# The head of a two-layer backbone kernel: filler products, block copies on ScalarE, squares summed by TensorE

## Chip, cores, metric

The kernel runs on one core of a Trainium2 chip. The metric is the device time of one execution in microseconds, as a median over runs.

## What is computed

One inference step of a hybrid backbone: two layers, the same weights for 128 context tokens and 128 latent tokens. Each layer is a half-step SwiGLU network, three token-mixing branches, and another half-step SwiGLU network. What matters here is how the first of these begins:

```
mod = silu(cond) @ w_ada[l] + b_ada[l]          # shift, scale, gate: 9 x 1024 per group
h = rmsnorm(x, g[0]) * (1 + mod[1]) + mod[0]
x = x + 0.5 * mod[2] * swiglu(h, ffn_w_in[l, 0], ffn_w_out[l, 0])
```

Here cond is a vector of 1024 for each of the two groups, x is 256 x 1024, and ffn_w_in has 2 x 2816 columns.

## The kernel before, in words

Channels lie on partitions: x is eight channel tiles of 128 x 256 (256 tokens, two groups of 128). A weight tile is 128 output columns for all 1024 inputs, 128 x 1024 in f32, 512 KB. The products run in fp32r as three terms: a weight tile `raw` is split into a high part (`hi`, a cast on ScalarE, function emit_hi) and a low part (`lo`, a subtraction on VectorE, emit_lo), the activations too, and mm3 adds hi x hi, hi x lo and lo x hi. So one weight tile with eight channel tiles is 24 products of 128 x 258 (256 tokens and two columns that carry the shift). All weight tiles stream in one fixed sequence through four `raw` buffers; load_more issues them from SP's queue, and a load waits until the low part of the tile four places earlier is made. At most eight transfers are in flight, since each issue takes the semaphore of the eighth one before it.

The first SwiGLU network cannot start its products before the scale of a channel tile is known, which is a column of silu(cond) @ w_ada. That is the head (the code behind `load(cT, cT_d)`, from line 1686). The part of w_ada for scale and shift is cut into eight blocks of 1 MB (two buffers `big` from `wa`); block b holds scale and shift of channel tile b.

- All of x is loaded first, ScalarE squares it (xstat, tile `t1k`), VectorE adds the squares up in `sqa`, TensorE sums over partitions, VectorE, POOL and VectorE make the reciprocal root, and TensorE spreads it (norm_chain, rstd_diag, rstd_rows) into `rb`. `settle` puts this whole chain ahead of block 0 on TensorE's queue.
- block_mm(b): the block's products, silu(cond) as the stationary side, into the one accumulator `pa`; VectorE copies it to a `t1k` tile.
- block_feed(b): two selection products (`s<-cst,t1k`) turn the copied rows into columns; VectorE adds bias and one (`mods`), multiplies with the gain (`amod`) and writes the shift columns of the activations' high and low part; xfeed then makes the high part on ScalarE (`big<-x,amod`) and the low part on VectorE.
- Five weight tiles (T0) get an accumulator in the head already: three `pm` and two halves of `spare`. From step JOIN[t] on, tile t takes the products of those channel tiles whose feed is made (`done[t] <= step - 2`).

A step issues block_mm(step), then block_feed(step - 1), then the main products, up to channel tile step - 2, then the split of a further weight tile. Behind the ten steps, ffn_in goes on with the sixth weight tile. The list scheduler (class Pace) places side work there by modelled times; each engine runs its own instructions in the order in which they were issued.

Of the kernel before, what the change touches and what calls it, by code (L numbers as in the profile page):

```python
# [10 lines left out]
F32 = mybir.dt.float32  # L11
# [5 lines left out]
P = 128  # L17
D = 1024
# [22 lines left out]

ADA_DEPTH = 2
T0 = 5
JOIN = (0, 0, 3, 4, 5)
RAW_BUFS = 4
WH_BUFS = 5
WL_BUFS = 5
# [30 lines left out]
BR_LESS = (0, 0, 0, 0, 1, 1, 1, 1)  # L78
WO_LESS = (0, 0, 0, 0, 1, 1, 1, 1)
FO_LESS = (0, 0, 0, 0, 1, 1, 1)  # L80
LOADS = (2, 3, 4, 4)
PRE = 2
AHEAD = ("", "hl", "h", "lh", "")
T_SIDE = 3
T_SETUP = 6
YCUT = ((0, 2), (2, 2), (4, 2), (6, 2))
# [338 lines left out]
def backbone(ctx: ExitStack, tc: tile.TileContext, seq, wst, wada, wa0, wrow, xT_d, cT_d, cB_d, ck_d, cv_d, h0_d, prm_d, cst_d,  # L425
# [16 lines left out]
    def v3(t, a):  # L442
        return t.rearrange("p (a b) -> p a b", a=a)
# [14 lines left out]
    def tmp(tag, shape, dt=F32, bufs=None):  # L458
        return tp.tile(shape, dt, tag=tag, name=nm(tag), **({"bufs": bufs} if bufs else {}))
# [22 lines left out]
    def ps2():  # L482
        return grab("s2", pp.tile([P, 2, 512], F32, tag="s2", bufs=1, name=nm("s2")))
# [13 lines left out]
    def C(name):  # L497
        return cst[:, CST[name][0]:CST[name][1]]

    def R(l, name):  # L500
        return prm[l][:, PRM[name][0]:PRM[name][1]]
# [42 lines left out]
    def settle(cond):  # L544
        idle = 0
        while not cond():
            cand = [(s, lst) for lst, n in ((side["first"], 99), (side["gens"], CONC), (side["slow"], 99)) for s in lst[:n]]
            cand = [c for c in sorted(cand, key=lambda c: when(c[0]) - FIRST * (c[1] is side["first"])) if when(c[0]) < 1e8]
            idle = 0 if any(step_side(*c) for c in cand) else idle + 1
            assert idle < 3  # L550
# [7 lines left out]
    def misc(gen):  # L558
        add(gen, True)
# [5 lines left out]
    def load(out, src):  # L565
        nc.sync.dma_start(out=out, in_=src)
        pace.op("dma", out.free_size() * P * 4 / 360e3, [out], [])

    def load_more(limit):
        while st["load"] < min(limit, st["cap"]):  # L570
            i = st["load"]
            raws[i] = pace.slot("raw", RAW_BUFS, wp.tile([P, 1024], F32, tag="raw", bufs=RAW_BUFS, name=nm("raw")))
            load(raws[i], wst[i])
            st["load"] += 1
# [188 lines left out]
    def xstat(m):  # L763
        if m == 0:
            stat["acc"] = tmp("sqa", [P, NT], bufs=1)
            S.activation(out=stat["acc"], in_=x[:, 0], func=AF.Square)
            return lambda: None
        q = stat["sq"] = t1k()
        S.activation(out=q, in_=x[:, m], func=AF.Square)
        return lambda: V.tensor_tensor(out=stat["acc"], in0=stat["acc"], in1=q, op=ALU.add)  # L770

    def rstd_cols(ss, n, scale):
        v = tmp("rsv", [P, 8])
        V.tensor_scalar(out=v[:, :n], in0=ss, scalar1=scale, scalar2=EPS, op0=ALU.mult, op1=ALU.add)
        r = tmp("rsr", [P, 8])
        G.tensor_tensor(out=r[:, :n], in0=v[:, :n], in1=halfc[:, :n], op=ALU.pow)
        return r

    def rstd_diag(acc, scale, more=None):
        ps = ps1(2)  # L780
        for g in range(2):
            T_.matmul(ps[:, g:g + 1], lhsT=acc[:, g * P:(g + 1) * P], rhs=C("ones")[:, 0:1], start=True,
                      stop=more is None)
            if more is not None:
                T_.matmul(ps[:, g:g + 1], lhsT=more[:, g * P:(g + 1) * P], rhs=C("ones")[:, 0:1], start=False, stop=True)
        r = rstd_cols(ps, 2, scale)
        drop("s1", ps)
        dg = t1k()
        for g in range(2):
            V.tensor_scalar(out=dg[:, g * P:(g + 1) * P], in0=C("ident"), scalar1=r[:, g:g + 1], scalar2=None, op0=ALU.mult)  # L790
        return dg
# [10 lines left out]
    def norm_chain(box):  # L802
        yield "pe", stat["acc"], "s1"
        dg = rstd_diag(stat["acc"], 1.0 / D)
        yield "pe", dg, "s1"
        box["rb"] = rstd_rows(dg)
# [19 lines left out]
    def xfeed(m):  # L826
        l, n = feed["ln"]
        hi, lo = feed["hs"][m]
        if FEED_ACT and m < FEED_ACT:
            f = t1k()  # L830
            for g in range(2):
                sl = slice(g * P, (g + 1) * P)
                S.activation(out=f[:, sl], in_=x[:, m, sl], func=AF.Copy, scale=Amod[l][:, n, m, g:g + 1])
            S.copy(hi[:, :NT], f)
            return lambda: V.tensor_tensor(out=lo[:, :NT], in0=f, in1=hi[:, :NT], op=ALU.subtract)
        for g in range(2):
            sl = slice(g * P, (g + 1) * P)
            S.activation(out=hi[:, sl], in_=x[:, m, sl], func=AF.Copy, scale=Amod[l][:, n, m, g:g + 1])

        def finish():  # L840
            for g in range(2):
                sl = slice(g * P, (g + 1) * P)
                V.scalar_tensor_tensor(out=lo[:, sl], in0=x[:, m, sl], scalar=Amod[l][:, n, m, g:g + 1], in1=hi[:, sl],
                                       op0=ALU.mult, op1=ALU.subtract)
        return finish
# [811 lines left out]
    def ssd_norm(l, yv, yh, yl, box):  # L1657
# [25 lines left out]
            V.scalar_tensor_tensor(out=box["ts"][m], in0=box["ts"][m], scalar=1.0, in1=rb[:, :NT], op0=ALU.add, op1=ALU.mult)  # L1683
        box["done"] = True

    load(cT, cT_d)
    load(x, xT_d)
    load(cst[:, 0:CST_E], cst_d[:, 0:CST_E])
    load(prm[0], prm_d[0, :, 0:PRM_R])
    V.memset(silc, 0.0)  # L1690
    V.memset(halfc, -0.5)
    S.activation(out=silc[:, :, 0:2], in_=cT, func=AF.Silu)
    blocks = []

    def block_load():
        blocks.append([big(), big()])
        for h in range(2):
            load(blocks[-1][h], wa0[len(blocks) - 1, h])

    def split():  # L1700
        emit_hi()
        emit_lo()

    for n in LOADS[:-1]:
        load_more(n)
        block_load()
    load_more(LOADS[-1])
    feed_open(0, 0)
    for m in range(KD):
        xstat(m)()  # L1710
    box = {"rb": None}
    misc(norm_chain(box))
    split()
    split()
    settle(lambda: box["rb"] is not None)
    evs = {}

    def block_mm(b):
        ps = pada()
        for k in range(KD):  # L1720
            j = k % 4
            T_.matmul(ps[32 * j:32 * j + 32, :], lhsT=silc[:, k, :], rhs=blocks[b][k // 4][:, j * NT:(j + 1) * NT],
                      start=(k < 4), stop=(k >= 4))
        evs[b] = t1k()
        V.tensor_copy(evs[b], ps)
        blocks[b] = None

    def block_feed(b):
        ev = evs.pop(b)
        pt = ps1(4)  # L1730
        for h in range(2):
            T_.matmul(pt[:, 2 * h:2 * h + 2], lhsT=ev[:, h * P:(h + 1) * P], rhs=C("sel"), start=True, stop=True)
        sc = mods[0][:, 1, b, :]
        V.tensor_scalar(out=sc, in0=pt[:, 0:2], scalar1=R(0, "bada")[:, KD + b:KD + b + 1], scalar2=1.0, op0=ALU.add,
                        op1=ALU.add)
        sh = mods[0][:, 0, b, :]
        V.tensor_scalar(out=sh, in0=pt[:, 2:4], scalar1=R(0, "bada")[:, b:b + 1], scalar2=None, op0=ALU.add)
        drop("s1", pt)
        V.tensor_scalar(out=Amod[0][:, 0, b, :], in0=sc, scalar1=R(0, "gain")[:, b:b + 1], scalar2=None, op0=ALU.mult)
        hi, lo = feed["hs"][b]  # L1740
        V.tensor_copy(hi[:, NT:], sh)
        V.tensor_tensor(out=lo[:, NT:], in0=sh, in1=hi[:, NT:], op=ALU.subtract)
        xfeed(b)()

    spare = ps2()
    pre, ws = [], []
    done = {}
    for step in range(KD + 2):
        if step < KD:
            block_mm(step)  # L1750
            if len(blocks) < KD:
                block_load()
                if len(blocks) == KD:
                    st["cap"] = len(seq)
                    load_more(st["lo"] + RAW_BUFS)
        if 1 <= step <= KD:
            block_feed(step - 1)
        for t in range(T0):
            if step < max(2, JOIN[t]):
                continue  # L1760
            if t == len(pre):
                ws.append(tiles8(use(("fin", 0, 0, (t % 2) * KF + t // 2))))
                pre.append(pmain(NT + 2) if t < 3 else spare[:, t - 3, 0:NT + 2])
                done[t] = 0
            while done[t] <= step - 2:
                k = done[t]
                mm3(pre[t], ws[t][k:k + 1], feed["hs"][k:k + 1], k == 0, k == KD - 1)
                done[t] += 1
        if st["lo"] < T0 and step + 2 >= JOIN[st["lo"]]:
            split()  # L1770
        if step >= KD - 3:
            for what in AHEAD[step - KD + 3]:
                what = emit_hi() if what == "h" else emit_lo()
    while st["lo"] < T0 + PRE:
        if st["hi"] == st["lo"]:
            emit_hi()
# [54 lines left out]
```

## Time and profile before

| | |
|---|---|
| runs | 1559.09 us median of 3 (1557.94 to 1559.66) |
| the profiled execution's own time | 1558.1 us |
| its span | 1556.3 us |
| TensorE busy | 1524.8 us, 98% |
| VectorE busy | 1303.8 us, 84% |
| ScalarE busy | 863.2 us, 55% |
| bytes moved | 348.26 MB, 224 GB/s over the span |

PE is TensorE's products and PEld its weight loads, DVE is VectorE, ACT is ScalarE, SP is the queue that issues the transfers. Names such as `pm<-big,wh` read output<-inputs by the program's tiles, buffer numbers left out; all compute instructions have line 394, since a helper there records them. An f32 product (not fp32r) appears as several records, so a block's eight products are 16 records, two selection products four. The time of a busy TensorE is modelled at its ends, so from start to start is a safer measure than a duration.

### The profile page before, as it was taken

Reading aid. Unit: us, or ns where it says so; the run is one execution under the profiler, and the core shown is the slowest. Engines: PE = TensorE matmul, PEld = TensorE weight load, DVE = VectorE, ACT = ScalarE, POOL = GpSimd, SP = SyncE. Lnnn points to the kernel's source line nnn. Section 1 sums busy time; section 2 is a strip of 40 time slices with the busy share of each in tenths; the row PEclk is TensorE's granted clock in tenths of the full one; section 3 lists DMA queues with packets and bytes.
Section 4 is the critical chain, followed back from the end, with each engine's and each line's share of the span. In section 5 each row is a group of like instructions: output and inputs, shape, how many; then the busy total and the mean of one; then the engine's idle time right before and its main releaser. Section 6 shows DMA issues by size and latency. Waiting matters only on the chain.

```text
span 1556.3 us, 30558 instructions
## 1 busy us (share of the span) xinstructions
PE 1524.8 (98%) x11950; PEld 1429.2 (92%) x11950; DVE 1303.8 (84%) x2404; ACT 863.2 (55%) x1560; POOL 60.7 (4%) x65
## 2 busy tenths in 40 slices
PE   5999999999999999999999999999999999999997
PEld 4988889989989999899899998998898999999986
DVE  5777698986888988888989899898779899888754
ACT  3564447665577446644447544577556754565442
POOL 0000002000001000000001000110000010010000
PEclk9999999999999999999999999999999999999998
DMA  9688774554755666688765877555466567568652
GB/s 372 219 328 298 262 268 163 189 188 129 247 207 182 216 231 231 214 281 297 258 217 197 292 276 269 192 177 182 151 218 212 177 206 264 171 202 284 222 180 81
DMA packets 98736, 348.26 MB, mean 224 GB/s; under 512 B 10912, under 2 KB 14624, under 8 KB 98464
## 3 DMA queue, kind: packets, MB, share of 16 engines
q1 hardware_dynamic: 98592, 346.31, 65.2%
q8 instruction: 94, 1.54, 0.4%
q14 instruction: 50, 0.41, 0.1%
HBM read 342.07 MB, written 4.19 MB: 222 GB/s over the span
## 4 chain that ended last, share of the span: by engine, by line
PE 80%; issue 11%; DVE 5%; DMA 2%; ACT 1%; POOL 0%; DVEq 0%; POOLq 0%; SPq 0%
PE pm L394 72%; PE s L394 6%; DMA big<-wada 2%; PE pa L394 2%; DVE big L394 1%; DVE t1k L394 1%; DVE wl L394 1%; ACT big L394 1%; DVE wide L394 0%; DMA x<-xT 0%; ACT wh L394 0%; DVE sqa L394 0%; ACT L394 0%; POOL osr L394 0%; ACT rb L394 0%
## 5 line engine op out<-in xcount | busy, mean ns | idle before, releaser
L394 PE MATMUL pm<-big,wh 128*128 128x256 f32 (+2 forms) x6568 | 1294.1, 294 | 3.6 <-DVE big L394 2.1
L394 PEld LDWEIGHTS pm<-big,wh 128*128 128x128 f32 x6568 | 1029.8, 189 | 52.8 <-issue 20.2
L394 PE MATMUL pm<-big,wl 128*128 128x256 f32 (+1 forms) x3592 | 1004.9, 281 | 0.0
L394 PEld LDWEIGHTS pm<-big,wl 128*128 128x128 f32 x3592 | 676.6, 188 | 2.4
L394 DVE TENSOR_TENSOR wl<-raw,wh 128x1024 fp32r<-128x1024 f32 x481 | 586.2, 1223 | 9.4 <-ACT wh L394 8.9
L394 ACT CAST wh<-raw 128x1024 fp32r<-128x1024 f32 x481 | 501.5, 1047 | 136.9 <-PE pm L394 97.8
L394 DVE SCALAR_TENSOR_TENSOR big<-big,big 128x1024 f32<-128x1024 f32 x198 | 241.2, 1218 | 13.4 <-DMA big<-wrow 11.7
L394 ACT CAST big<-t1k 128x256 fp32r<-128x256 f32 x88 | 35.8, 407 | 155.8 <-DVE t1k L394 155.8
L394 PE MATMUL pm<-wh,big 128*128 128x512 f32 x256 | 89.0, 410 | 0.0
L394 ACT ACTIVATE big<-x,amod 128x128 fp32r<-128x128 f32 x96 | 33.4, 395 | 96.2 <-DVE x L394 77.8
L394 DVE TENSOR_TENSOR wide<-pm,rb 128x258 f32<-128x258 f32 (+1 forms) x108 | 45.1, 421 | 38.8 <-PE pm L394 32.9
L394 DVE SCALAR_TENSOR_TENSOR x<-pm,mods,x 128x128 f32<-128x128 f32 x152 | 43.5, 343 | 35.7 <-PE pm L394 35.7
L394 ACT COPY big<-pm 128x256 f32<-128x256 f32 (+2 forms) x88 | 31.0, 373 | 56.6 <-PE pm L394 55.9
L394 PEld LDWEIGHTS pm<-wh,big 128*128 128x128 f32 x256 | 48.1, 188 | 13.2 <-issue 2.3
L394 DVE TENSOR_TENSOR big<-t1k,big 128x256 fp32r<-128x256 f32 x128 | 55.5, 437 | 1.6 <-ACT big L394 0.9
L394 ACT ACTIVATE t1k<-wide 128x128 f32<-128x128 f32 (+1 forms) x96 | 33.4, 395 | 37.7 <-DVE wide L394 37.7
L394 PE MATMUL pm<-wl,big 128*128 128x512 f32 x128 | 50.6, 395 | 0.0
L394 ACT ACTIVATE t1k<-pm 128x256 f32<-128x256 f32 x58 | 22.3, 385 | 47.3 <-PE pm L394 47.2
L394 PE MATMUL s<-big,big 128*64 128x128 f32 (+5 forms) x416 | 46.4, 312 | 0.0
L394 POOL TENSOR_TENSOR rsr<-rsv,halfc 128x2 f32<-128x2 f32 x9 | 6.3, 698 | 917.5 <-DVE rsv L394 917.5
L394 DVE SCALAR_TENSOR_TENSOR big<-big,cw,big 128x252 f32<-128x252 f32 (+1 forms) x96 | 39.3, 472 | 2.6 <-ACT big L394 2.5
L394 PEld LDWEIGHTS s<-big,big 128*128 128x128 f32 (+2 forms) x416 | 35.3, 172 | 5.5 <-issue 3.3
(150 smaller groups left out, 970.4 us busy)
## 6 DMA issues: line engine op xcount, KB each, us to landing
raw<-wst SPq DMA_DIRECT2D x486, 512.0 KB, 4.3
big<-wrow SPq DMA_DIRECT2D x96, 512.0 KB, 5.7
big<-wada SPq DMA_DIRECT2D x32, 512.0 KB, 5.8
big<-wa SPq DMA_DIRECT2D x16, 512.0 KB, 10.1
big<-cB SPq DMA_DIRECT2D x12, 512.0 KB, 7.3
x<-xT SPq DMA_DIRECT2D x1, 1024.0 KB, 5.1
big<-h SPq DMA_DIRECT2D x2, 512.0 KB, 5.1
ns<-t SPq DMA_DIRECT2D x8, 128.0 KB, 3.7
```

The lines of the kernel that those rows point to most:

```text
L394: r = fn(*a, **k)
```

## The change

It rewrites the head. The norm's chain is no longer ahead of block 0. Instead the squares of x are made one or two at a time behind the blocks' feeds (table XSTAT), and TensorE sums each over partitions with a ones column into one accumulator `pq`; the root and its spreading come at steps 7 and 8. A step now issues block_mm(b), main products up to channel tile b - 1, the selection and feed of the same block b, then squares and their ones products, then products of a zero tile into an accumulator that is not read (table WARM: 13 ahead of block 0, then 9, 6 and 2). The copy of the accumulator moves from VectorE to ScalarE. Shift and scale get their bias in one VectorE operation, and one plus scale is taken inside the product with the gain. x is loaded in four pieces between the blocks (ORDER), the parameters ahead of them. Weight tiles join at steps 1, 2, 3, 7 and 8.

```diff
-JOIN = (0, 0, 3, 4, 5)
-LOADS = (2, 3, 4, 4)
-AHEAD = ("", "hl", "h", "lh", "")
+JOIN = (1, 2, 3, 7, 8)
+ORDER = "wxrwxrwxrwx wr wr w w".split()
+WARM = (13, 9, 6, 2)
+XSTAT = {1: (0,), 2: (1, 2), 3: (3, 4), 4: (5,), 5: (6,), 6: (7,)}
+AHEAD = {6: "h", 7: "l", 8: "hl"}
...
+    zero = tmp("t512", [P, 512], F32R)
+    V.memset(zero.bitcast(F32), 0.0)
     load(cT, cT_d)
-    load(x, xT_d)
+    load(prm[0], prm_d[0, :, 0:PRM_R])
     load(cst[:, 0:CST_E], cst_d[:, 0:CST_E])
-    load(prm[0], prm_d[0, :, 0:PRM_R])
...
+    spare = ps2()
+
+    def warm(n):
+        for _ in range(n):
+            T_.matmul(spare[:, 1, :], lhsT=zero[:, 0:P], rhs=zero, start=True, stop=True)
...
-    for m in range(KD):
-        xstat(m)()
     box = {"rb": None}
-    misc(norm_chain(box))
-    split()
-    split()
-    settle(lambda: box["rb"] is not None)
...
         evs[b] = t1k()
-        V.tensor_copy(evs[b], ps)
+        S.copy(evs[b], ps)
...
-    def block_feed(b):
+    def block_feed(b, lo_too):
...
-        sc = mods[0][:, 1, b, :]
-        V.tensor_scalar(out=sc, in0=pt[:, 0:2], scalar1=R(0, "bada")[:, KD + b:KD + b + 1], scalar2=1.0, op0=ALU.add,
-                        op1=ALU.add)
-        sh = mods[0][:, 0, b, :]
-        V.tensor_scalar(out=sh, in0=pt[:, 2:4], scalar1=R(0, "bada")[:, b:b + 1], scalar2=None, op0=ALU.add)
+            T_.matmul(pt[:, 2 - 2 * h:4 - 2 * h], lhsT=ev[:, h * P:(h + 1) * P], rhs=C("sel"), start=True, stop=True)
+        sh, sc = mods[0][:, 0, b, :], mods[0][:, 1, b, :]
+        V.tensor_tensor(out=mods[0][:, 0:2, b, :], in0=v3(pt, 2),
+                        in1=R(0, "bada").rearrange("p (i k) -> p i k", k=KD)[:, 0:2, b:b + 1].to_broadcast([P, 2, 2]), op=ALU.add)
         drop("s1", pt)
-        V.tensor_scalar(out=Amod[0][:, 0, b, :], in0=sc, scalar1=R(0, "gain")[:, b:b + 1], scalar2=None, op0=ALU.mult)
+        V.scalar_tensor_tensor(out=Amod[0][:, 0, b, :], in0=sc, scalar=1.0, in1=R(0, "gain")[:, b:b + 1].to_broadcast([P, 2]),
+                               op0=ALU.add, op1=ALU.mult)
...
-        xfeed(b)()
+        later = xfeed(b)
+        if lo_too:
+            emit_lo()
+        later()
...
+    pq = ps1(2)
+    warm(WARM[0])
+    for step in range(KD + 1):
+        if step < KD:
+            block_mm(step)
+            if step + 1 < len(ORDER):
+                head_load(ORDER[step + 1])
...
+        joined(step)
+        if step == KD:
+            box["rb"] = rstd_rows(dg)
+            for t in range(len(pre)):
+                mains(t, KD - 1)
+        for t in range(len(pre)):
+            mains(t, step)
+        if step == KD - 1:
+            dg = diag(pq, 1.0 / D)
+        if step < KD:
+            if step < T0:
+                emit_hi()
+            block_feed(step, step < T0)
+            for m in XSTAT.get(step, ()):
+                q = t1k()
+                S.activation(out=q, in_=x[:, m], func=AF.Square)
+                for g in range(2):
+                    T_.matmul(pq[:, g:g + 1], lhsT=q[:, g * P:(g + 1) * P], rhs=C("ones")[:, 0:1], start=(m == 0 and g == 0),
+                              stop=(m == KD - 1), skip_group_check=True)
+        if step + 1 < len(WARM):
+            warm(WARM[step + 1])
```

The function mains(t, n) issues mm3 for weight tile t up to channel tile n - 1; joined(step) gives tile t its accumulator once step has reached JOIN[t]; diag is the second half of rstd_diag.

How the order on an engine moves is read at two places. First TensorE, in the middle of the head. Before, from the products of block 5 (`pa`, eight products in two rows) on: `s_359` is the selection of block 4, and the `pm` rows are main products of weight tiles 0, 1 and 2 with channel tile 3.

```order
L394 MATMUL pa_348<-big_223,silc 32x256 x4
L394 MATMUL pa_348<-big_224,silc 32x256 x4
L394 MATMUL s_359<-cst,t1k_304 128x2 x2
L394 MATMUL pm_239<-big_113,big_140 128x258
L394 MATMUL pm_239<-big_115,big_140 128x258
L394 MATMUL pm_239<-big_113,big_142 128x258
L394 MATMUL pm_243<-big_113,big_146 128x258
L394 MATMUL pm_243<-big_115,big_146 128x258
L394 MATMUL pm_243<-big_113,big_148 128x258
```

The same engine in the change: the second row of block 5's products, the nine main products of channel tile 4, block 5's own selection (`128x2`) and the ones products of a square (`128x1`).

```order
L396 MATMUL pa_377<-big_192,silc 32x256 x4
L396 MATMUL pm_197<-big_122,big_156 128x258
L396 MATMUL pm_197<-big_124,big_156 128x258
L396 MATMUL pm_197<-big_122,big_167 128x258
L396 MATMUL pm_241<-big_122,big_201 128x258
L396 MATMUL pm_241<-big_124,big_201 128x258
L396 MATMUL pm_241<-big_122,big_212 128x258
L396 MATMUL pm_295<-big_122,big_251 128x258
L396 MATMUL pm_295<-big_124,big_251 128x258
L396 MATMUL pm_295<-big_122,big_262 128x258
L396 MATMUL s_397<-cst,t1k_386 128x2 x2
L396 MATMUL s_125<-cst,t1k_408 128x1 x2
```

The selection has moved from ahead of the main products to behind them and belongs to the same block as the products above; the ones products are new, and the next block's products follow them.

Second ScalarE, in the middle of the head. Before, between the spreading of the norm and block 4's feed (`big<-x,amod` is a feed, `big<-raw` a weight tile's high part):

```order
L394 COPY rb_162<-s_160 128x256
L394 ACTIVATE big_113<-x,amod_84 128x128 x2
L394 CAST big_208<-raw_101 128x1024
L394 ACTIVATE big_113<-x,amod_84 128x128 x2
L394 CAST big_247<-raw_107 128x1024
L394 ACTIVATE big_113<-x,amod_84 128x128 x2
L394 CAST big_291<-raw_144 128x1024
L394 ACTIVATE big_113<-x,amod_84 128x128 x2
L394 ACTIVATE big_114<-x,amod_84 128x128 x4
```

In the change, from block 4's copy to block 6's square (`t1k<-pa` is a copy of the accumulator, `t1k<-x` a square):

```order
L396 COPY t1k_345<-pa_336 128x256
L396 CAST big_356<-raw_195 128x1024
L396 ACTIVATE big_122<-x,amod_84 128x128 x2
L396 ACTIVATE t1k_373<-x 128x256
L396 COPY t1k_386<-pa_377 128x256
L396 ACTIVATE big_122<-x,amod_84 128x128 x2
L396 ACTIVATE t1k_408<-x 128x256
L396 COPY t1k_421<-pa_412 128x256
L396 ACTIVATE big_122<-x,amod_84 128x128 x2
L396 ACTIVATE t1k_443<-x 128x256
```

The copies are new on this engine, and each square stands behind the feed of its block and ahead of the next block's copy.

## Rows read from the trace of the kernel before

**Rows 1.** The page: busy time, share of the span and instructions of each engine.

```profile
PE 1524.8 (98%) x11950; PEld 1429.2 (92%) x11950; DVE 1303.8 (84%) x2404; ACT 863.2 (55%) x1560; POOL 60.7 (4%) x65
```

**Rows 2.** The chain of waits in order of time, 0 to 110 us: start, us, what.

```profile
1.18 5.14 DMA x<-xT
...
10.62 1.22 DVE big L394 x2
...
15.62 1.91 PE pa L394 x16
...
26.11 1.23 DVE big L394
27.34 0.35 DVE t1k L394
...
47.03 20.33 PE pm L394 x168
```

**Rows 3.** The timeline of TensorE, 10 to 47 us: start, us, engine, line, operation.

```profile
10.76 1.01 PE L394 MATMUL s<-cst,sqa 128*128 128x1 f32 x4 [10.76 <-DVE sqa L394]
14.39 1.22 PE L394 MATMUL s<-t1k,cst 128*128 128x256 f32 x2 [2.63 <-DVE rb L394]
15.55 1.94 PE L394 MATMUL pa<-big,silc 128*32 128x256 f32 x16
18.03 1.68 PE L394 MATMUL pa<-big,silc 128*32 128x256 f32 x16 [0.55 <-DVE t1k L394]
...
24.08 1.07 PE L394 MATMUL pa<-big,silc 128*32 128x256 f32 x16 [1.27 <-DVE t1k L394]
...
39.49 1.07 PE L394 MATMUL pa<-big,silc 128*32 128x256 f32 x16
40.49 0.61 PE L394 MATMUL s<-cst,t1k 128*128 128x2 f32 x4
40.96 1.33 PE L394 MATMUL pm<-big,big 128*128 128x258 f32 x9
42.12 0.88 PE L394 MATMUL s<-big,big 128*128 128x258 f32 x6
42.84 0.50 PE L394 MATMUL s<-cst,t1k 128*128 128x2 f32 x4
...
46.87 0.41 PE L394 MATMUL pm<-big,wh 128*128 128x258 f32 x2
```

**Rows 4.** The timeline of VectorE, one block's feed.

```profile
43.38 0.34 DVE L394 TENSOR_SCALAR mods<-s,prm 128x2 f32<-128x2 f32 x2 [0.44 <-PE s L394]
43.64 0.22 DVE L394 TENSOR_SCALAR amod<-mods,prm 128x2 f32<-128x2 f32 x1
...
44.33 0.64 DVE L394 SCALAR_TENSOR_TENSOR big<-x,amod,big 128x128 fp32r<-128x128 f32 x2 [0.21 <-ACT big L394]
44.89 1.22 DVE L394 TENSOR_TENSOR wl<-raw,wh 128x1024 fp32r<-128x1024 f32 x1
46.02 0.42 DVE L394 TENSOR_TENSOR wide<-pm,rb 128x258 f32<-128x258 f32 x1
```

**Rows 5.** The timeline of ScalarE: squares, a copy from the accumulator, a feed, a cast.

```profile
6.66 2.37 ACT L394 ACTIVATE t1k<-x 128x256 f32<-128x256 f32 x7
...
15.65 0.37 ACT L394 COPY rb<-s 128x256 f32<-128x256 f32 x1 [4.74 <-PE s L394]
...
43.89 0.69 ACT L394 ACTIVATE big<-x,amod 128x128 fp32r<-128x128 f32 x2 [0.41 <-DVE amod L394]
44.49 1.03 ACT L394 CAST wh<-raw 128x1024 fp32r<-128x1024 f32 x1
```

**Rows 6.** Three windows: us, busy time of each engine, granted clock, DMA share, GB/s.

```profile
0.00:10.00 10.00, 0.00 (x0) 0.00 (x0) 2.67 (x8) 5.13 (x12) 0.20 (x4) 1.00 0.79 283
10.00:20.00 10.00, 6.07 (x42) 2.98 (x42) 4.06 (x10) 1.29 (x2) 0.70 (x1) 1.00 1.03 415
20.00:30.00 10.00, 8.21 (x88) 5.92 (x87) 7.46 (x27) 4.89 (x9) 0.00 (x0) 1.00 1.02 413
```

**Rows 7.** The timeline of SP's queue: the first issue behind eight transfers that waits for the fifth.

```profile
8.50 1.60 SPq L566 DMA_DIRECT2D big<-wa  x2
```

More of the change, by code (lines that the diff above doesn't have):

```diff
@@ L785, in rstd_diag, with diag @@
                 T_.matmul(ps[:, g:g + 1], lhsT=more[:, g * P:(g + 1) * P], rhs=C("ones")[:, 0:1], start=False, stop=True)
+        return diag(ps, scale)
+    def diag(ps, scale):
         r = rstd_cols(ps, 2, scale)
@@ L1692, in backbone @@
     S.activation(out=silc[:, :, 0:2], in_=cT, func=AF.Silu)
+    spare = ps2()
+    def warm(n):
+        for _ in range(n):
+            T_.matmul(spare[:, 1, :], lhsT=zero[:, 0:P], rhs=zero, start=True, stop=True)
     blocks = []
+    xs_in = [0]
     def block_load():
@@ L1702, in split, with head_load @@
         emit_lo()
[L1704 to L1707, printed above, removed]
+    def head_load(items):
+        for c in items:
+            if c == "w":
+                block_load()
+            elif c == "x":
+                i = xs_in[0]
+                load(x[:, i:i + 2], xT_d[:, i:i + 2])
+                xs_in[0] = i + 2
+            else:
+                st["cap"] += 1
+                load_more(st["cap"])
+    st["cap"] = 0
+    head_load(ORDER[0])
     feed_open(0, 0)
-    for m in range(KD):
-        xstat(m)()
     box = {"rb": None}
-    misc(norm_chain(box))
-    split()
-    split()
-    settle(lambda: box["rb"] is not None)
     evs = {}
@@ L1731, in block_feed @@
         for h in range(2):
-            T_.matmul(pt[:, 2 * h:2 * h + 2], lhsT=ev[:, h * P:(h + 1) * P], rhs=C("sel"), start=True, stop=True)
-        sc = mods[0][:, 1, b, :]
-        V.tensor_scalar(out=sc, in0=pt[:, 0:2], scalar1=R(0, "bada")[:, KD + b:KD + b + 1], scalar2=1.0, op0=ALU.add,
-                        op1=ALU.add)
-        sh = mods[0][:, 0, b, :]
-        V.tensor_scalar(out=sh, in0=pt[:, 2:4], scalar1=R(0, "bada")[:, b:b + 1], scalar2=None, op0=ALU.add)
+            T_.matmul(pt[:, 2 - 2 * h:4 - 2 * h], lhsT=ev[:, h * P:(h + 1) * P], rhs=C("sel"), start=True, stop=True)
+        sh, sc = mods[0][:, 0, b, :], mods[0][:, 1, b, :]
+        V.tensor_tensor(out=mods[0][:, 0:2, b, :], in0=v3(pt, 2),
+                        in1=R(0, "bada").rearrange("p (i k) -> p i k", k=KD)[:, 0:2, b:b + 1].to_broadcast([P, 2, 2]), op=ALU.add)
         drop("s1", pt)
-        V.tensor_scalar(out=Amod[0][:, 0, b, :], in0=sc, scalar1=R(0, "gain")[:, b:b + 1], scalar2=None, op0=ALU.mult)
+        V.scalar_tensor_tensor(out=Amod[0][:, 0, b, :], in0=sc, scalar=1.0, in1=R(0, "gain")[:, b:b + 1].to_broadcast([P, 2]),
+                               op0=ALU.add, op1=ALU.mult)
         hi, lo = feed["hs"][b]
@@ L1742, in block_feed, with joined @@
         V.tensor_tensor(out=lo[:, NT:], in0=sh, in1=hi[:, NT:], op=ALU.subtract)
-        xfeed(b)()
-    spare = ps2()
+        later = xfeed(b)
+        if lo_too:
+            emit_lo()
+        later()
     pre, ws = [], []
     done = {}
[L1748 to L1757, printed above, removed]
+    def joined(step):
         for t in range(T0):
-            if step < max(2, JOIN[t]):
+            if step < JOIN[t]:
                 continue
@@ L1764, in backbone, with mains @@
                 done[t] = 0
[L1765 to L1773, printed above, removed]
+    def mains(t, upto):
+        while done[t] < upto:
+            k = done[t]
+            mm3(pre[t], ws[t][k:k + 1], feed["hs"][k:k + 1], k == 0, k == KD - 1)
+            done[t] += 1
+    pq = ps1(2)
[5 more added lines that the diff above has]
+                head_load(ORDER[step + 1])
+                if len(blocks) == KD:
+                    st["cap"] = len(seq)
+                    load_more(st["lo"] + RAW_BUFS)
+        joined(step)
[19 more added lines that the diff above has]
+            warm(WARM[step + 1])
+        for what in AHEAD.get(step, ""):
+            what = emit_hi() if what == "h" else emit_lo()
     while st["lo"] < T0 + PRE:
```

## The prediction

> **What bounds the kernel now.** I read the page first: TensorE is busy 98% of the span [rows 1]. Then the chain of waits in order of time, to see where the other 2% lie [rows 2]: up to 47 us it changes engine all the time (input transfer, VectorE, TensorE), and from 47.03 on it is TensorE without a break, 168 products of a weight tile in 20.33 us. So the kernel is a head of 47 us and a body that TensorE alone sets. The order of the instructions on all engines is the same in both kernels behind the head (TensorE's sixth weight tile is the first common piece). So I compare one mark: the start of the sixth tile, 46.87 us [rows 3]. What the mark gains or loses, the kernel gains or loses.
>
> The head is eight blocks, and how often a block comes round is read from TensorE's timeline [rows 3]: block 0 at 15.55, block 7 at 39.49, that is 3.42 us each. A block's evacuation, its selection products and its feed overlap the next block there: the selection of block b-1 stands behind the products of block b, and TensorE runs on without waiting for the feed it has just set off.
>
> **The change, part by part.** The blocks' order on TensorE becomes: products of block b, main products of channel tile b-1, selection of block b, ones products of the squares, products of block b+1. The ones products wait for a square that ScalarE makes *behind* block b's feed, and the feed waits for VectorE's scale, which waits for the selection. Nothing is pipelined any more, and one round is the sum of its parts:
> - products of a block to the next instruction: 1.00 (39.49 to 40.49 [rows 3]);
> - nine main products: 40.96 to 42.12, 1.16 [rows 3];
> - selection to VectorE's first operation: 42.84 to 43.38, 0.54 [rows 3, 4];
> - VectorE's scale and shift: 43.38 to ScalarE's start at 43.89 is 0.51 with three operations [rows 4, 5]; the change has two, about 0.13 less with a wider first one, so I take 0.42;
> - ScalarE's feed until the next instruction starts: 43.89 to 44.49, 0.60; a square, 0.40 (seven in 2.37 are 0.33 from start to start, and the last one's end) [rows 5];
> - hand-over to TensorE 0.06 (the gaps between a product's end and its reader are of this size), and the ones products, the same form as the selection but for one column, 0.60 until the next block.
>
> Sum: 1.00 + 1.16 + 0.54 + 0.42 + 0.60 + 0.40 + 0.06 + 0.60 = **4.78 us** a round, against 3.42 before. It counts for blocks 2 to 7 (rounds 1 to 6 have squares).
>
> *Start.* The norm of all of x leaves the front, where it held block 0 until 15.55. Now block 0 waits for its own load: 1.33 MB lie ahead of its end, with 0.28 MB of it small inputs. By 10 us 283 GB/s have brought 2.83 MB, then it is 415 GB/s [rows 6]. Block 1 ends at 3.16 MB: 10.8 us. The queue's issue at 8.50 waited for the fifth transfer (1.85 MB, due at some 7.6 by these rates) [rows 7], so landings come 0.8 us behind the byte count: 11.6. Whether block 0's products run cold (1.94) or warm (1.00) [rows 3] changes nothing, since they begin near 7 and block 1 is not there before 11.6. So the 13 filler products at the start, and the nine after block 0, I cost at nothing: the load of block 1 hides them.
>
> *Block 2.* The first square stands behind feed 1, which stands behind the cast of the second raw tile: 3.95 MB, 12.7 + 0.8 = 13.5; cast 1.03, feed 0.60, square 0.40, hand-over and ones 0.66 give 16.2; six fillers of 512 columns at 1.16 / 9 x 512 / 258 = 0.26 give 17.7. *Block 3:* 4.78 + a second square and pair of ones (0.33 + 0.14) + two fillers 0.5 = 5.75: 23.5. *Block 4:* 15 main products for nine (+0.77), two squares (+0.47): 6.0: 29.5. *Blocks 5 to 7:* 3 x 4.78: **43.8** for block 7, against 39.49. Its load is not what it waits for: 12.34 MB ahead of its end, 2.83 + 4.15 by 20 us, the other 5.36 at 413 GB/s: 33.0, with 0.8 added 33.8.
>
> *End.* Behind block 7: its products 1.00, main products of the three joined tiles (9), of tile 3 (21), selection 0.5, the product that spreads the norm 0.6 (1.22 for it before, cold [rows 3]), tile 4 (21), the last channel of all five (15). 66 x 20.33 / 168 = 8.0, in all 10.1 us. The mark falls at **53.9**, where the old tail took 46.87 - 39.49 = 7.4: tiles 3 and 4 joined at steps 4 and 5 and now join at 7 and 8. Hidden in it: feed 7 (0.42 + 0.69 + 0.64 [rows 4, 5]) behind tile 4's 2.5; scale of the norm with its POOL operation behind the 3.6 of tile 3; the two weight splits and the first evacuation (1.03 + 1.22 + 0.42, just under the 4.4 of 36 products) before the mark. If that cover fails it costs some tenths.
>
> The block copies on ScalarE (0.37 for 0.42 [rows 5]) lie behind the main products and cost nothing; without those it would be +0.43 a round. VectorE loses the copies and seven additions, and is not the bound. Three more DMA issues cost SP 0.4 each, while eight transfers are in flight.
>
> Mark 53.9 - 46.87 = +7.0 us; I take +6.8, as the fillers may be nearer 0.22. The profiled execution took 1558.1 us (span 1556.3 and 1.8 around it), 1.0 below the median of the runs, 1559.09; so the median goes to **1565.9 us**. Bounds of the round: 4.4, if selection, hand-over and ones are each at their shortest row (0.47 apart instead of 0.60), to 5.1; times six, -2.3 and +1.9. The start is good to 1 us either way.
>
> **TensorE's order.** The whole loss hangs on a wait for ScalarE at the ones products holding up block b+1, which has long landed. The row at 24.08 shows TensorE standing 1.27 us on a block's evacuation with other work queued behind it [rows 3]. The Trainium skill, TensorE: Matmul & The Clock Gate, section Step-by-step: what each phase is for, says that matmuls stay in program order and only weight loads are drawn ahead; by that rule the forecast stands, and without it the first rival's 1557 would come. No row of this trace tells the two apart for such a wait.
>
> **The rivals.**
> 1. *Loads set the pace (not slower).* If the squares don't hold TensorE, because ScalarE gets to them during the next block's time, a round is 1.00 + 1.16 + 0.6 + 0.6 = 3.4 us; with 2.8 for fillers and the six further products, block 7 starts at 34.8, one us behind its landing. With the same tail the mark is 44.9: -2.0, **1557.1 us**. It decides from the point where the round falls below (46.87 - 10.1 - 11.6 - 3.5) / 6 = 3.6, 3.5 being what blocks 2 to 4 take above six equal rounds. For it: the squares need only x, which is there. Against: the order on ScalarE puts each square behind its block's feed. Chance 0.11.
> 2. *Shorter rounds.* Waits of the six rounds come out at 4.0 to 4.3, with less hand-over than the rows show: +2 to +4, **1562 us**. Chance 0.13.
> 3. *The clock falls.* In a round of 4.78 TensorE stands idle some 1.5 us, between selection and ones. The granted clock is 1.00 in each stretch [rows 6], yet block 1 took 1.68 and later blocks 1.07 [rows 3], so the lower of the two levels is seen in the first products only. At the lower one a block is +0.65, nine products up to +1.1, selection and ones +0.4 each (1.01 for four cold, 0.61 warm [rows 3]): 2.5 a round over four rounds, and some 2 in the tail: **1578 us**. For it: more idle time than before. Against: the 1.27 at 24.08 did not bring it. The Trainium skill, same page, section HAM oscillation — how this bites in real kernels, describes waits between groups of products that bring the low clock back each time; by it this rival would come if 1.5 us is enough of a wait, and the trace shows it only for a shorter one. Chance 0.09.
> 4. *It doesn't matter.* Were the body bound by loads behind the head, the mark would count for little. TensorE's chain without a break [rows 2] excludes that nearly: **1559 us**, 0.02.
>
> **How the numbers follow.** Forecast 0.65, rival 1 0.11, rival 2 0.13, rival 3 0.09, rival 4 0.02. A measurement of this kernel can tell about 0.2% from no change, 3.1 us: 1556.0 to 1562.2. Faster by more needs rival 1 with rounds that follow the loads without a rest, or a shorter tail than I have: 0.10. Within: the rest of rival 1 and of rival 4, and two thirds of rival 2: 0.14. Slower: 0.76. The range reaches from rival 2's low end to the forecast with its longest rounds and a little clock loss: 1560.5 to 1570.5, which leaves out rivals 1 and 3.
>
> **What would show it.** In the changed profile: block 1's products near 11.6 us, block 7's near 43.8, the sixth tile's first product near 53.9; blocks 4 to 7 4.8 us apart; TensorE's wait before each ones product ended by ScalarE's square, some 1.5 us each. Wrong if block 7 follows its load at 33.8 (rival 1), or if block products in rounds 3 to 6 take over 1.5 us (rival 3).

## The result, and the profile after

The change is slower: 1576.33 us, median of 4 runs (1573.41 to 1577.09), against 1559.38 (4 runs of before on the same chip). The ratio is 1.011, with a 95% interval of 1.0095 to 1.0125. The forecast was 1565.9 us with a range of 1560.5 to 1570.5: right in sign, 10.4 us short, and outside its range. What came is the third rival, the one with the falling clock, at 1578 us and a chance of 0.09.

The profiled execution took 1577.07 us with a span of 1575.3, 19.0 longer than before. In the page's first part TensorE is busy 23.4 us longer than in [rows 1]:

```profile
PE 1548.2 (98%) x12008; PEld 1447.8 (92%) x12008; DVE 1297.4 (82%) x2382; ACT 867.4 (55%) x1568; POOL 60.7 (4%) x65
```

The 30 zero products, most of them where TensorE stood idle before, take 11.9 us of that (5.91 + 2.33 + 2.44 + 1.20 by the timeline), and the ones products of the squares take 5.9 us where the one sum over partitions took 1.0 [rows 3]. The rest is much the same work that took longer. Where, the timeline of TensorE shows (start, us, engine, line, operation; in brackets the idle time before it and what ended it), the answer to [rows 3]:

```profile
11.62 0.64 PE L396 MATMUL pa<-big,silc 128*32 128x256 f32 x8
12.70 0.64 PE L396 MATMUL pa<-big,silc 128*32 128x256 f32 x8 [0.44 <-DMA big<-wa]
...
16.63 0.61 PE L396 MATMUL s<-cst,t1k 128*128 128x1 f32 x4 [2.19 <-ACT t1k L396]
...
27.23 1.94 PE L396 MATMUL pa<-big,silc 128*32 128x256 f32 x16
...
40.63 0.60 PE L396 MATMUL s<-cst,t1k 128*128 128x1 f32 x4 [1.48 <-ACT t1k L396]
41.17 1.62 PE L396 MATMUL pa<-big,silc 128*32 128x256 f32 x16
42.72 2.30 PE L396 MATMUL pm<-big,big 128*128 128x258 f32 x9
44.82 0.57 PE L396 MATMUL s<-cst,t1k 128*128 128x2 f32 x4
46.88 0.61 PE L396 MATMUL s<-cst,t1k 128*128 128x1 f32 x4 [1.48 <-ACT t1k L396]
...
53.79 1.93 PE L396 MATMUL pa<-big,silc 128*32 128x256 f32 x16
...
65.87 0.40 PE L396 MATMUL pm<-big,wh 128*128 128x258 f32 x2
...
69.90 0.47 PE L396 MATMUL pm<-big,wh 128*128 128x258 f32 x2 [0.99 <-DVE wide L396]
```

Block 1 starts at 11.62, block 7 at 53.79, and the mark, the sixth tile's first product, lies at 65.87 against 46.87 before: 19.0 later, as much as the span grew. Behind the mark, by the table of waits, TensorE waits 1.6 us longer for evacuations (2.9 for 1.3, of which the row at 69.90 is 0.99) and 2.2 us less for the second layer's w_ada (1.0 for 3.2), which roughly cancels. So the loss is in the head.

The loop that the prediction describes is there. The chain of waits (start, us, what) runs through one round:

```profile
22.58 0.35 PE s L396 x4
...
22.96 0.17 DVE mods L396
...
23.16 0.17 DVE amod L396
...
23.35 0.70 ACT big L396 x2
24.05 0.32 ACT t1k L396
...
24.41 2.89 PE s L396 x10
```

Selection, scale, feed, square and ones products follow each other, and from 22.93 to 24.41 TensorE does nothing. The table of waits (TensorE, 0 to 72 us: in total, times, longest) has 10.1 us of this kind over the head. 9.6 of them are six waits for squares, and 0.50 is the selection of block 0 waiting for the copy of its accumulator, which writes a `t1k` tile too:

```profile
PE s L396 <- ACT t1k L396: 10.1, 7, 2.2
```

The new part is the column PEclk, the granted clock, in windows of the same execution (columns as in [rows 6], which had 1.00 everywhere):

```profile
10.00:15.00 5.00, 4.00 (x31) 2.29 (x29) 2.37 (x8) 2.39 (x5) 0.00 (x0) 1.00 1.02 413
...
25.00:30.00 5.00, 5.00 (x28) 3.08 (x29) 0.26 (x1) 0.71 (x2) 0.00 (x0) 0.50 1.03 415
...
45.00:50.00 5.00, 3.52 (x32) 2.83 (x31) 1.21 (x6) 1.38 (x4) 0.00 (x0) 0.84 0.01 3
50.00:55.00 5.00, 3.52 (x24) 2.80 (x26) 1.49 (x8) 1.94 (x4) 0.70 (x1) 0.50 0.00 2
...
60.00:65.00 5.00, 5.00 (x42) 4.95 (x42) 3.54 (x10) 1.91 (x4) 0.00 (x0) 1.00 0.07 11
```

Half clock is 1.2 of 2.4 GHz. It is granted in five stretches from 17.7 to 58.6 us, each begun within 2 us behind the end of a wait for a square, and there a block takes 1.93 us instead of 1.07 and nine main products 2.30 instead of 1.33. In the fourth row almost no bytes move any more (DMA share 0.00): the blocks have long landed, and TensorE is slow by itself.

### The profile page after: what moved, and what is told of

It is laid out like the page before. It is cut to its first block, busy times and chain, and to the rows that moved or that the text cites. A ratio compares the mean times of both kernels' runs of the same rounds, so it can differ in the third digit from the quotient of the medians.

```text
span 1575.3 us, 30662 instructions
## 1 busy us (share of the span) xinstructions
PE 1548.2 (98%) x12008; PEld 1447.8 (92%) x12008; DVE 1297.4 (82%) x2382; ACT 867.4 (55%) x1568; POOL 60.7 (4%) x65
## 4 chain that ended last, share of the span: by engine, by line
PE 78%; issue 12%; DVE 6%; DMA 2%; ACT 2%; SPq 0%; POOL 0%; DVEq 0%; POOLq 0%; ACTq 0%
PE pm L396 69%; PE s L396 7%; DVE wl L396 2%; PE pa L396 2%; DVE t1k L396 2%; DVE big L396 1%; DMA big<-wada 1%; ACT big L396 1%; DMA raw<-wst 1%; DMA big<-cB 0%; DVE wide L396 0%; ACT wh L396 0%; SPq L568 0%; ACT t1k L396 0%; POOL osr L396 0%
```

## The experiments

All ratios are to the kernel before, run on the same chip; "mark" is the start of the sixth weight tile in the profiled execution.

| run | ratio (95% interval) | block 7 | mark |
|---|---|---|---|
| the change | 1.0110 (1.0095 to 1.0125) | 53.79 | 65.87 |
| e1_fill_wait | 1.0052 (1.0039 to 1.0065) | 44.81 | 54.73 |
| e11_half_filled | 1.0075 (1.0060 to 1.0089) | 45.92 | 55.83 |
| e2_late_ones | 1.0026 (1.0009 to 1.0044) | 43.12 | 54.34 |
| e3_vector_sums | 1.0028 (1.0012 to 1.0045) | 41.07 | 54.78 |
| e4_no_filler | 1.0126 (1.0097 to 1.0155) | 52.26 | 64.44 |
| e5_late_ones_and_casts | 1.0012 (1.0003 to 1.0022) | 37.56 | 48.47 |
| e7_copies_alone | 0.9998 (0.9989 to 1.0007) | 41.42 | 48.81 |
| e8_filler_alone | 1.0009 (1.0000 to 1.0018) | 44.01 | 51.39 |
| e10_copies_and_filler | 1.0001 (0.9990 to 1.0011) | 38.95 | 46.37 |
| e6_rebuilt | 0.9992 (0.9984 to 1.0001) | 37.26 | 45.66 |
| e9_weights_earlier | 1.0031 (1.0019 to 1.0042) | 44.39 | 52.41 |
| e12_third_cast | 0.9986 (0.9977 to 0.9995) | 37.30 | 45.72 |

### Is it the clock, or the wait?

**e1_fill_wait** leaves the serial round as it is, and fills the wait:

```diff
             block_feed(step, step < T0)
+            if step in XSTAT:
+                warm(6)
             for m in XSTAT.get(step, ()):
```

> The mark is the start of the sixth weight tile: 46.87 us before, 65.87 in the change. Theory 1: the 1.5 us in which TensorE waits for a square in each round brings its clock down, and the low clock costs some 12 of the 19 us. Six zero products put into that wait (1.3 us of work at the high clock) then keep the granted clock at 1.00, rounds take 4.8 us as in the forecast, and the mark falls at 54 +- 2: 1564 to 1568 us. Theory 2: the clock falls because of what the head's products are (blocks with 32 columns, zero operands), not because of the wait. Then it stays as low, the fillers take 2.6 us at the low clock and stick out of the wait by 1.1, six times: 1580 us or more.

TensorE's timeline, one round and the mark, then a window with the granted clock (columns as in [rows 6]):

```profile
42.29 0.50 PE L396 MATMUL s<-cst,t1k 128*128 128x2 f32 x4
42.65 1.64 PE L396 MATMUL s<-t 128*128 128x512 f32 x6
44.28 0.61 PE L396 MATMUL s<-cst,t1k 128*128 128x1 f32 x4
44.81 1.07 PE L396 MATMUL pa<-big,silc 128*32 128x256 f32 x16
...
54.73 0.40 PE L396 MATMUL pm<-big,wh 128*128 128x258 f32 x2
```

```profile
30.00:40.00 10.00, 10.00 (x85) 7.60 (x84) 4.04 (x16) 3.70 (x9) 0.00 (x0) 1.00 0.93 371
```

The square is ready no earlier, yet with six zero products in the wait the granted clock stays at 1.00, a block takes 1.07, a round 4.70 to 4.73 (forecast 4.78), and the mark comes at 54.73 (forecast 53.9). 11.1 us of the mark's 19.0 were the clock; the other 7.9 are the start and the serial rounds at the high clock, forecast at 7.0. It is not an accident of the profiled execution: the mean granted clock of a whole execution is 0.989 to 0.992 in the four runs of the change, 0.995 to 0.998 in the nine of e1, and 0.996 to 0.998 in those of the kernel before. The time fell by less, 8.5 us by the medians. In the profiled execution the span is +10.9 for a mark of +7.9. A part of that difference is the clock again: in the body TensorE waits 2.72 us for w_ada, until 665.32, and behind it the clock is at half until 668.7, which it is not before.

**e11_half_filled** is the same with warm(3).

> The changed kernel with three zero products, not six, ahead of the squares' ones products: the wait of 1.49 us a round is filled by some 0.7 and 0.8 stays. Theory (the clock falls only when TensorE rests longer than that): granted clock 1.00 in the head, blocks of 1.07, rounds 4.7 to 4.8, sixth tile near 54.5, 1565 to 1568 us, ratio 1.004 to 1.006. Rival (any rest in each round brings it down): blocks of 1.6 to 1.9 in some rounds, mark 58 to 66, 1570 to 1577 us.

```profile
8.75 0.64 PE L396 MATMUL pa<-big,silc 128*32 128x256 f32 x8 [0.52 <-DMA big<-wa]
9.88 0.61 PE L396 MATMUL s<-cst,t1k 128*128 128x2 f32 x4 [0.49 <-ACT t1k L396]
10.35 3.89 PE L396 MATMUL s<-t 128*128 128x512 f32 x9
...
40.67 0.61 PE L396 MATMUL s<-cst,t1k 128*128 128x1 f32 x4 [0.69 <-ACT t1k L396]
41.21 1.07 PE L396 MATMUL pa<-big,silc 128*32 128x256 f32 x16
```

With 0.69 us of rest left in each round every block takes 1.07: filling half is enough. The clock did fall once, earlier: in the first block TensorE rested 0.28, 0.52 and 0.49 us, and the nine zero products behind took 3.89 us instead of 2.31. That costs 1.6 us, and the mark is 1.1 later than in e1. So the clock of 1.00 that was expected for the whole head is missed at this place, and the run is at 1569.99 us, 2 above the range expected.

**e4_no_filler** sets WARM = (0,), no zero products at all.

> All filler products are taken away, the rest is the change. Theory 1: the fillers are outside the waits that matter; without them blocks 2 and 3 start some 2 us earlier and the clock falls as before, perhaps a round earlier: 1572 to 1577 us. Theory 3: the fillers of steps 1 and 2, which hold up blocks 2 and 3 and run at the low clock, are a main cost of the change (2.4 and 1.2 us in its trace, and what follows): 1570 us or less.

```profile
32.51 1.07 PE L396 MATMUL s<-cst,t1k 128*128 128x1 f32 x8 [1.48 <-ACT t1k L396]
33.51 1.93 PE L396 MATMUL pa<-big,silc 128*32 128x256 f32 x16
```

It is as slow as the change (mark 64.44, waits of 1.48, blocks from the third on up to 1.93), at 1580.33 us even 3 above the range expected. The fillers don't cost the loss, and where they stand they don't prevent it: they are at the start of the head, while the rest is in the rounds behind.

### Taking the wait away

**e2_late_ones** issues the ones products behind the next block's products.

```diff
             block_mm(step)
+            while late:
+                m, q = late.pop(0)
+                for g in range(2):
+                    T_.matmul(pq[:, g:g + 1], lhsT=q[:, g * P:(g + 1) * P], rhs=C("ones")[:, 0:1], ...
```

> The ones products of a square are issued behind the next block's products, so that TensorE no longer stands until the square is made. Theory 1: a round becomes products 1.00, a wait of 0.45, ones 0.6, main products 1.16, selection 0.54, in all 3.75 us; the clock holds, since waits are under 1 us; block 7 starts near 37 and the mark falls at 46 to 49: 1558 to 1562 us. Theory 2: rounds get shorter by the wait, but at the low clock (blocks 1.9, nine main products 2.2): 5.5 us a round, mark near 58, 1570 us.

```profile
29.16 1.05 PE L396 MATMUL s<-cst,t1k 128*128 128x1 f32 x8 [1.89 <-ACT t1k L396]
...
31.94 1.93 PE L396 MATMUL pa<-big,silc 128*32 128x256 f32 x16
```

Block 4 came at 26.21 instead of 35.07. Then there is one new wait of 1.89 us; behind it the clock fell and three blocks took 1.93. The square was late because ScalarE stood in front of it on another wait (its timeline):

```profile
27.16 1.04 ACT L396 CAST big<-raw 128x1024 fp32r<-128x1024 f32 x1 [3.62 <-DMA raw<-wst]
```

The change casts a weight tile in each of the first five steps, ahead of the feed. Once the rounds are short the fourth tile (tile 3, counted from 0) has not landed, and feed, square and ones products queue behind its cast. So neither range came: the rounds were short up to block 4 and slow behind it, with the mark at 54.34 and 1562.98 us.

**e3_vector_sums** takes the ones products out of the rounds: VectorE adds the squares up, as before (xstat and rstd_diag).

> Squares stay where the change has them, but VectorE adds them up as in the kernel before, and TensorE takes two ones products in all. Theory 1: a round is products 1.00, a wait for the feed of 0.8 (1.4 where VectorE makes a low part), main products 1.16, selection 0.5: 3.5 to 4.1 us; block 7 near 36.5, mark at 46 to 48: 1558 to 1561 us. Theory 2: clock low in spite of it, 1566 to 1572 us.

```profile
28.83 0.56 PE L396 MATMUL pm<-big,big 128*128 128x258 f32 x1 [2.30 <-ACT big L396]
...
48.43 0.67 PE L396 MATMUL s<-t1k,cst 128*128 128x256 f32 x2 [1.20 <-DVE mods L396]
48.75 4.38 PE L396 MATMUL s<-big,big 128*128 128x258 f32 x21
```

No ones product waits in the rounds, but a main product does, 2.30 us at 28.83, for the feed behind the same cast. The clock falls there (1.93 and 1.68 for blocks 5 and 6). It falls a second time behind a wait of 1.20 at the spreading of the norm, where 21 products take 4.38 us (2.88 in the change, at 61.34). The mark is at 54.78 and the time 1565.00 us, between the two ranges expected. Both kernels without the ones' wait are thus stopped by the next one, the cast; that their marks agree to 0.5 us is chance, since block 7 came 2 us earlier here.

**e5_late_ones_and_casts** is e2 with the casts and splits of tiles 3 and 4 one step later: `split_now = step in (0, 1, 2, 4, 5)` in place of `step < T0`.

> The run with the late ones products stood 1.89 us in round 4, behind the cast of a weight tile that had not landed, and its clock fell there. Here tiles 3 and 4 are cast and split one step later as well. Theory 1 (the clock falls after a wait of about that length): no wait over 1 us is left from block 2 on, the granted clock stays at 1.00, block 7 starts at 37 to 39, and the mark falls at 47.5 to 49.5: 1559.5 to 1562 us, and the kernel is not faster than before. Theory 2 (the head's products don't keep the clock up): blocks 5 to 7 still take 1.9 us each and the mark stays at 54.

```profile
35.14 0.60 PE L396 MATMUL s<-cst,t1k 128*128 128x1 f32 x4 [0.48 <-ACT t1k L396]
...
37.56 1.07 PE L396 MATMUL pa<-big,silc 128*32 128x256 f32 x16
```

Rounds of 4.0 us, rests of 0.48, clock 1.00 throughout, the mark 17.4 us earlier than in the change. This confirms that the order of two groups of instructions, the ones products and the casts, made nearly all of the loss (17.4 of the mark's 19.0). It is still 0.1% slower than before.

### What the parts are worth in the kernel before

**e7_copies_alone** puts only the block copies on ScalarE and takes scale and shift in two operations. **e8_filler_alone** is the kernel before with the copies and operations as they were, and with 32 zero products ahead of the norm's sum over partitions and 12 ahead of its spreading.

> The kernel before, with the change's block copies on ScalarE and its two VectorE operations for scale and shift, and nothing else. In the head before, VectorE sets the rounds that make a low part (copy, bias, gain, two shifts, the low part of the feed and of a weight tile: 3.65 us from copy to copy). Without the copy and one operation that is 3.0, and TensorE's own 3.4 sets the pace: block 7 some 1 to 2 us earlier, mark at 45 to 46, 1557 to 1558 us. Rival: copies queue behind ScalarE's casts and nothing is won, 1559 us.

> The kernel before with filler alone: 32 zero products ahead of the norm's sum and 12 between the sum and its spreading. Blocks 0 and 1 then take 1.0 us each (1.94 and 1.68 before) and the spreading 0.6 (1.22). Theory 1: as VectorE sets the next rounds, up to 1.5 us of this reach the mark: 1557.5 to 1559 us. Rival: the fillers themselves hold up the norm's products, 1560 us.

Both fall short of what was expected. The times, 1557.50 and 1558.69 us, lie in the ranges given, but the kernel before itself ran at 1557.90 beside them, so nothing is gained; and the marks, 48.81 and 51.39, are later than before instead of earlier. The first blocks do come faster (in e8 blocks 0 and 1 take 1.07 for 1.94 and 1.68 [rows 3]), and then TensorE stands before data that have not landed: 0.64 and 0.51 us in e7, 1.66 in e8. Behind that the clock falls, to 0.50 between 25 and 31 us in e7. TensorE in e7, then in e8:

```profile
23.95 0.92 PE L394 MATMUL pa<-big,silc 128*32 128x256 f32 x8 [0.51 <-DMA big<-wa]
...
25.67 2.93 PE L394 MATMUL pm<-big,big 128*128 128x258 f32 x12
28.53 1.94 PE L394 MATMUL pa<-big,silc 128*32 128x256 f32 x16
```

```profile
25.02 0.64 PE L394 MATMUL pa<-big,silc 128*32 128x256 f32 x8 [1.66 <-DMA big<-wa]
```

**e10_copies_and_filler** tests this cause: e7 with 3 and 6 zero products behind blocks 1 and 2.

> The kernel before with the block copies on ScalarE and the two-operation scale and shift, as in the run of that part alone, and 3 and 6 zero products behind blocks 1 and 2, where that run waited 0.64 and 0.51 us for loads ahead of block 3. Theory (a clock that falls behind thinly filled stretches cost that run its gain): the load wait is filled, blocks 3 and 4 take 1.07 instead of up to 1.94 us, twelve products 1.5 instead of 2.93, sixth tile near 45 to 46.5 instead of 48.81: 1555.5 to 1557 us, ratio 0.9985. Rival (the clock of that stretch comes from something else than the waits for loads): clock 0.50 near 25 to 31 us again, mark 48.8 or later, ratio 1.000 or above.

```profile
24.09 1.07 PE L394 MATMUL pa<-big,silc 128*32 128x256 f32 x16
25.09 0.61 PE L394 MATMUL s<-cst,t1k 128*128 128x2 f32 x4
25.56 1.69 PE L394 MATMUL pm<-big,big 128*128 128x258 f32 x12
27.18 1.07 PE L394 MATMUL pa<-big,silc 128*32 128x256 f32 x16
```

Nine products that compute nothing take 2.4 us off the mark: it falls from 48.81 to 46.37, and the clock is 1.00 throughout. The time did not follow: by the table of waits the body of this execution waits 4.0 us for w_ada of the second layer (1.2 in e7), and 1.0001 is no difference. So the clock's part is confirmed and the time expected is missed. As what the body waits there lies between 0.6 and 4.0 us in the profiled executions (0.6 in the rebuilt head, 3.2 before), a mark that moves by as much can't be read from the time.

### A rebuilt head

**e6_rebuilt** joins what held: squares added by VectorE, casts one step later, only the first weight tile's products ahead of the selection, the other tiles' behind it (they run while the feed is made), tiles 3 and 4 joined at steps 5 and 7. It also has five zero products in place of the last two, and the splits of the sixth and seventh tile at step 7 (AHEAD).

> What the runs so far say put together: the change's loads, copies and operations, VectorE's sums of the squares (no ones products in the rounds), the feed of a block hidden behind main products of the block before it, tiles 3 and 4 split one step later, tile 3 joined at step 5 and tile 4 at 7. TensorE's work from block 1 at 11.6 us on is 7 blocks, 8 selections, 120 products and the norm, some 27 us, with 3 to 4 us of waits for loads: mark at 42 to 45, 1554.5 to 1557.5 us, faster than before. If theory 1 misses something that holds the head up, 1559 us or more.

```profile
49.77 0.48 PE L396 MATMUL pm<-big,wh 128*128 128x258 f32 x2 [1.08 <-DVE wide L396]
```

Clock 1.00, mark 45.66, 20.2 us before the change's but over the range expected. The time, 1556.32 us, is in its range, and yet "faster than before" is not shown: the interval reaches 1.0001. A wait of 1.08 us is left at 49.77, where VectorE's evacuation stands behind two low parts.

**e9_weights_earlier** is the rebuilt head with weight tiles moved ahead of the last blocks (ORDER, JOIN = (1, 2, 3, 4, 4), splits at steps 0 to 3 and more of them in AHEAD).

> The rebuilt head with the weight tiles ahead of the last blocks in the order of the loads, joined at steps 1, 2, 3, 4 and 4, and split at the first steps, so that the seventh tile's split comes in time. Theory (TensorE's order and its cover set the mark, loads no longer do): blocks keep 1.07 us, no wait of 1.1 us at the seventh weight tile, sixth tile near 44 to 45 us (45.66 in the rebuilt head), 1553.5 to 1555.5 us, ratio 0.997 to 0.998. Rival (loads set the pace now): the last blocks' data come later, TensorE waits for them, the clock falls with it, block 7 near 39 or later and the mark near 46 to 48: 1557 to 1560 us.

The rival came, and stronger than expected (mark 52.41 and 1562.55 us, for 46 to 48 and 1557 to 1560). Blocks now arrive later, and TensorE (timeline) waits 2.14 us for block 4; the clock falls to 0.50 and 24 products behind it take 5.11 us, where the rebuilt head needs 3.01:

```profile
27.33 0.64 PE L396 MATMUL pa<-big,silc 128*32 128x256 f32 x8 [2.14 <-DMA big<-wa]
...
31.96 5.11 PE L396 MATMUL s<-big,big 128*128 128x258 f32 x24
```

**e12_third_cast** is the rebuilt head again, with its loads as they were, and moves one cast, AHEAD = {7: "hlhlh"} for "hlhl".

> The rebuilt head with one cast more (the high part of the eighth weight tile) ahead of the copy of the spread norm on ScalarE, where that engine stood idle 1.57 us. Theory (the 1.08 us that TensorE waited at 49.77 for an evacuation was the VectorE queue behind that late cast, and what the head loses or gains the kernel does): sixth tile at 45.7 as before, the wait of 1.08 falls to 0.0 to 0.3 us, span some 1.0 shorter, 1555.2 to 1556 us on this ratio: 0.998 to 0.999. Rival (the wait only moves to the tiles behind): total idle of TensorE between 45 and 65 us unchanged, ratio as in the rebuilt head, 0.9985 to 1.000.

```profile
48.68 0.48 PE L396 MATMUL pm<-big,wh 128*128 128x258 f32 x2
```

The wait is gone (the row of the rebuilt head began at 49.77), and it has not moved to the tiles behind, which was the rival: between 45 and 65 us TensorE is busy for all of the 20 us, 18.92 in the rebuilt head. The span is only 0.7 us shorter, as the wait for the second layer's w_ada is 1.9 us here and was 0.6. 1555.70 us against 1558.23: the ratio 0.9986 is below 1 with its whole interval, though by less than the prediction's 0.2%. It is the lowest ratio of the kernels here; that it is faster than the rebuilt head is not shown by the times, whose intervals overlap.

## Why the prediction was right and wrong

**Right: the path.** The blocks' order on TensorE is serial as described, TensorE stays in program order, and ones products hold up a block that has landed. By the rule of the Trainium skill, TensorE: Matmul & The Clock Gate, section Step-by-step: what each phase is for, the forecast was to stand, and the trace agrees: 1.48 or 1.49 us of standing in each round (forecast 1.5) with the next block's products queued behind. In the change the mark and the span grew by the same 19.0 us, as forecast; in the other runs the two differ by up to some 3 us (e7: mark +1.9, span -0.7; e1: +7.9 and +10.9).

**Luck: the start.** Block 1 begins at 11.62 as forecast (11.6), but not for the reason given. Nine zero products end there (9.37 and 2.33 long), and the second half of the block, on which the forecast of 11.6 rested, is waited for until 12.70. The second raw tile is as late: its cast begins at 14.63, for 13.5, and so the first wait is 2.19. Both came some 1.1 us later than the byte count and its 0.8 us gave.

**Right: the sum at the high clock.** With the clock held (e1) rounds are 4.7 and the mark is 54.73, for 4.78 and 53.9.

**Wrong: the terms of the round, which is the step that failed.** "Products of a block to the next instruction: 1.00", "nine main products: 1.16", selection and ones 0.54 and 0.60 were all taken from rows at the high clock and used for all six rounds. In the change the three rounds forecast at 4.78 took 6.10, 6.24 and 6.38. From block 1 to block 7 the rounds exceed the forecast by 10.0 us (53.79 for 43.8), and the tail by 2.0 (12.1 for 10.1). Of the 10.0 e1 keeps 1.0 with the clock held (block 7 at 44.81), about the late landing above; the other 9.0 are the low clock. The prediction had this case, with 10 and 2 as its price, and gave it 0.09. That the 10 fits is in part luck: it was 2.5 a round in four rounds, and what came is 1.3 to 2.0 above the forecast in each of six. What it held against it, that a wait of 1.27 us [rows 3] did not bring the clock down, is true of that one wait and carried too far. Before, it was one wait; in the change it was one in each round. That the number of waits makes the difference is not shown: in e3 one wait of 1.20, in a stretch that was otherwise filled, did bring the clock down. The Trainium skill, same page, section HAM oscillation — how this bites in real kernels, describes waits between groups of products that bring the low clock back each time. The trace agrees that they do; it differs in the length, as the waits of the page's example are for loads and longer, and here 1.48 or 1.49 us in each round was enough.

**Wrong in a small term: the cover of the splits.** "If that cover fails it costs some tenths": it cost 0.99 us at 69.90, behind the mark, for the evacuation of the first accumulator.

**Not settled: the copies.** That they would be +0.43 a round on VectorE was not tried in the change. With the shorter scale and shift in the kernel before they give no time that can be measured (0.9998): the first blocks come faster and then wait for a load, and behind that the clock falls.

## What to carry to other kernels

Before adding an instruction that waits, find what stands behind it in its engine's queue, and price the round as a sum if all of it is on one path. If TensorE then rests in each round, price the round at the low clock too, and don't let one harmless wait in the old trace decide; a few zero products in the rest, or other products moved into it, are what the runs showed to help. Where loads arrive at a fixed rate, as in this head (some 410 GB/s), starting earlier only moves the rest to the loads, so fill that one as well.

## What the runs showed that was not expected

- Length of one rest does not tell whether the clock falls. It held behind 1.27 us before [rows 3], behind 0.69 in each round (e11) and 0.48 in each (e5). It fell behind 1.49 in each round, and behind rests of 1.66 (e8), 1.89 (e2), 2.14 (e9) and 2.30 (e3), but also behind 1.20, less than the 1.27 that did no harm (e3, at 48.43), and behind 0.64 and 0.51 us close together (e7).
- Not even the same rests tell: around the first block TensorE rested 0.28, 0.52 and 0.49 us in e11 and the clock fell; in e1 it rested 0.82 and 0.49 there, as much in all, and nine zero products took 2.31 us; in e12 it rested 0.67, 0.55 and 0.49, more in all, and they took 2.33. What tips it was not settled.
- Products of zeros kept the clock up (e1: 1.00 from 10 to 50 us with six in each round).
- The column of the granted clock is not enough by itself. It reads 1.00 in e4 from 15 to 25 us, though a block there takes 1.93 us and nine main products 2.30, as at half clock elsewhere. The same holds for block 0 of the kernel before, 1.94 us at a column of 1.00 [rows 3, 6]. The time of a known piece of work has to be read beside it.
